# Token-major gates and merge, and transposes by 32x32 blocks and DMA over DRAM, in a hybrid encoder block

## The chip, the cores and the metric

The kernel runs on one core of a Trainium2 chip. The metric is the device time of one execution in microseconds (us); lower is better. The median of the runs shown is 1886.4 us. Everything is computed in float32 precision; the large products are done as three products of split operands (see below).

## The reference

The block takes `x` (256 tokens, 2048 channels) and computes, with one weight matrix `w_in` for all first projections:

```python
proj = h @ w_in                      # q, k, v, r, af, ab, hy_u, gate_logits
y_gla = gated_linear_attention(q, k, v, r, af, ab)     # 4 heads, both directions
y_hy = hyena(hy_u)                   # short conv, then two long convolutions by FFT
g = sigmoid(gate_logits)             # two gates of 2048 channels
merged = g[0] * (y_gla @ w_gla_o) + g[1] * (y_hy @ w_hy_o)
h = layernorm(ALPHA * h + merged @ w_out)
ff = square(relu(h @ w_ff1)) @ w_ff2                   # 2048 -> 8192 -> 2048
out = layernorm(ALPHA * h + ff)
```

## The kernel before

**Products.** Each activation is kept as `act[128, kt, 2, 256]`: channels on partitions (16 tiles `kt` of 128 channels), a high and a low part, and 256 tokens. `split_hi_lo` (L107) makes the parts: a cast on ScalarE (L108) and a subtraction on VectorE (L109). Weights arrive in 305 blocks of 128 x 2048 numbers in the order of use (`wblk`, built by `_layout`), each as one DMA on SP's queue, and are split in two halves in the same way (`fetch`, L115). There is room for three raw blocks and three split halves. A product is high x high + high x low + low x high.

There are two forms of product:
- `channel_pair` (L175): the weights are the stationary operand and the activation moves. A block holds 128 output channels by all 2048 inputs. It takes 16 matmuls of 512 columns (high and low activations side by side) and 16 of 256. The result has channels on partitions; the two sides are added by `channel_sum` (L169): a copy on ScalarE (L172) and an addition on VectorE (L173).
- `token_group` (L202): the activation is stationary and the weights move. Four blocks hold 512 outputs, and each block takes 24 matmuls of 512 columns. The result has tokens on partitions, in two PSUM banks, ready to use.

**Stages, in order.** First gates and filters: ga, q, k (channel), r (token), with the filters of Hyena computed on the side. Then v (token) with the GLA heads on the side: `gla_gates`, `gla_scores`, `gla_out` (L587). Then g1, the first gate (channel), whose sigmoid is applied in place after the GLA pool is closed (L642). Then the Hyena stage: eight chunks of 256 channels, each with three channel pairs uv, ux, uz, and, spread by `go_after` (L754), the eight channel pairs go of `y_gla @ w_gla_o`. Then g2 (channel), ho (`y_hy @ w_hy_o`, channel, merged into `mT`), wo (token), layer norm, and the MLP: ff1 in quarters (channel, L969), ff2 in quarters (token, L996), in the order f0, f1, w0, f2, w1, f3, w2, w3.

**Side work.** `later(d, fn)` puts a function on a list; `pump()` is called once per weight block and runs what is due, so `d` counts blocks from the call. Within what is written, the order of each engine is set by a planner that works with its own costs for every instruction and DMA; on the chip each engine then takes its instructions in that order. TensorE, VectorE, ScalarE, and the DMA queues of SP, ScalarE and POOL are all such in-order queues.

**Transposes.** Four places turn a tile between channels and tokens on partitions, each with four or eight 128x128 TensorE transposes against an identity into a side PSUM bank: `yt` in `gla_out` (L608), `vt` and `x1t` in `to_tokens` (L660), `yT` at the end of `hy_inv` (L737). These are 32 transposes each.

**Hyena chunk.** `hy_v` splits the turned v; `hy_fwd` loads the filter `Tl` from DRAM on POOL's queue and makes the forward transform `Zp`; `hy_mul` (L698) is the product in the frequency domain on VectorE; `hy_inv` the inverse `yp`, multiplied with x1 (order 0) or x2 (order 1). The result `yo` goes to DRAM (`yd`, L741) and comes back before ho as `yr` (L782).

Of the kernel before, what the change touches and what calls it, by code (L numbers as in the profile page):

```python
# [10 lines left out]
F32 = mybir.dt.float32  # L11
F32R = mybir.dt.float32r
I32 = mybir.dt.int32
AF = mybir.ActivationFunctionType
# [45 lines left out]
def block_kernel(  # L60
# [151 lines left out]
    def rsqrt_eps(dst, src, scale, pool, name, between=lambda: None):  # L212
# [4 lines left out]
        eng.scalar.activation(y, t, AF.Exp, scale=-0.5)  # L217
# [4 lines left out]
        eng.vector.tensor_tensor(dst, y, t, op=ALU.mult)  # L222

# [363 lines left out]
    def gla_out(h):  # L587
        def run():
            sth, stl = hst.pop(("st", h))
            vh, vl = v_sb.pop(h)  # L590
            y = gp.tile([P, NT, 512], F32, tag="y", name=f"y{h}")
            for ib in range(NT):
                po = psum_side(f"o{h}{ib}")
                for jb in range(NT):
                    cs = slice(ib * P, (ib + 1) * P)
                    mm3(po, sth[:, jb, cs], stl[:, jb, cs], vh[:, jb], vl[:, jb], jb == 0, jb == 1)
                ss = gp.tile([P, 1], F32, tag="ss", bufs=2, name=f"ss{h}{ib}")
                rs = gp.tile([P, 1], F32, tag="rsd", bufs=2, name=f"rs{h}{ib}")
                nc.scalar.activation(y[:, ib, :], po, AF.Square, accum_out=ss)
                rsqrt_eps(rs, ss, 1.0 / 512.0, gp, f"rq{h}{ib}")  # L600
                nc.vector.scalar_tensor_tensor(
                    y[:, ib, :], po, rs, g_sb[:, ib, h * 512:(h + 1) * 512], op0=ALU.mult, op1=ALU.mult)
            for k2 in range(2):
                pt = psum_side(f"yt{h}{k2}")
                for kk in range(2):
                    for ib in range(NT):
                        kt = 2 * k2 + kk
                        nc.tensor.transpose(  # L608
                            pt[:, kk * L + ib * P:kk * L + (ib + 1) * P],
                            y[:, ib, kt * P:(kt + 1) * P], ident)  # L610
                s = slice(4 * h + 2 * k2, 4 * h + 2 * k2 + 2)
                split_hi_lo(yT[:, s, 0], yT[:, s, 1], pt.rearrange("p (a b) -> p a b", a=2))
        return run

    for h in range(HEADS):
# [9 lines left out]
        later(1, gla_out(h))  # L625
# [3 lines left out]
        qp.tile([P, 8, L], F32, tag="q", name="m0"),  # L629
        qp.tile([P, 8, L], F32, tag="k", name="m1"),  # L630
    ]

    def m_pair(c2):
        return m_sb[c2 // 4][:, 2 * (c2 % 4):2 * (c2 % 4) + 2, :]

    for c2 in range(8):
        channel_pair(xT, f"g1_{c2}", m_pair(c2))
    drain()
    gstk.close()
    for c2 in range(8):  # L640
        mp = m_pair(c2)
        nc.scalar.activation(mp, mp, AF.Sigmoid)  # L642
# [17 lines left out]
    def to_tokens(src, name):  # L660
        pt = psum_side(name)
        for c in range(2):
            for tb in range(NT):
                nc.tensor.transpose(pt[:, tb * CW + c * P:tb * CW + (c + 1) * P], src[:, c, tb * P:(tb + 1) * P], ident)
        return pt.rearrange("p (a b) -> p a b", a=2)
# [5 lines left out]
    def hy_v(c):  # L671
        def run():
            z = z_tiles(f"{c}0")
            split_hi_lo(z[0], z[1], to_tokens(cst.pop(("v", c)), f"vt{c}"))
            cst[("z", c, 0)] = z
        return run

    def hy_x1(c):
        def run():
            x1 = hp.tile([P, NT, CW], F32, tag="x1", name=f"x1_{c}")  # L680
            nc.scalar.copy(x1, to_tokens(cst.pop(("x1c", c)), f"x1t{c}"))
            cst[("x1", c)] = x1
        return run
# [34 lines left out]
    def hy_inv(c, o):  # L718
        def run():
# [5 lines left out]
            if o == 0:  # L725
                zf = hp.tile([P, NT, CW], F32, tag="zf", name=f"zf{c}")
                nc.vector.tensor_tensor(zf, py3, cst.pop(("x1", c)), op=ALU.mult)
# [3 lines left out]
            else:  # L731
                zf = hp.tile([P, NT, CW], F32, tag="zf", name=f"zg{c}")
                nc.scalar.copy(zf, py3)
                pt = psum_side(f"yT{c}")
                for cc in range(2):
                    for tb in range(NT):
                        nc.tensor.transpose(pt[:, cc * L + tb * P:cc * L + (tb + 1) * P], zf[:, tb, cc * P:(cc + 1) * P], ident)  # L737
                yo = hp.tile([P, 2, L], F32, tag="zf", name=f"yo{c}")
                nc.vector.tensor_tensor(yo, pt.rearrange("p (a b) -> p a b", a=2), cst.pop(("x2", c)), op=ALU.mult)
                yd = drp.tile([P, 2, L], F32, tag=f"yd{c}", name=f"yd{c}")  # L740
                nc.gpsimd.dma_start(yd, yo)  # L741
                yh_dram[c] = yd
# [4 lines left out]
    def gla_o_pair():  # L747
        c2 = go_done[0]
        go_done[0] += 1
        ps = channel_pair(yT, f"go{c2}")  # L750
        mp = m_pair(c2)
        nc.vector.tensor_tensor(mp, mp, ps, op=ALU.mult)

    go_after = [0, 0, 1, 1, 1, 1, 1, 3]  # L754
    for c in range(NCH):
# [14 lines left out]
        for _ in range(go_after[c]):  # L770
            gla_o_pair()
# [403 lines left out]
```

## Time and profile before

| | |
|---|---|
| median of three runs | 1886.4 us (1885.57 to 1888.03) |
| profiled execution, span from first to last instruction | 1881.2 us |
| TensorE busy | 1862.4 us (99%), 9852 matmuls |
| VectorE busy | 1313.7 us (70%) |
| ScalarE busy | 948.2 us (50%) |
| POOL | 30.8 us (2%), 61 instructions |
| DMA | 375 MB, mean 199 GB/s |

The page of the profile gives for the profiled execution its span alone; the median of the runs is 5.2 us above it. "Busy" is the time in which an engine executes something. A row of the windows gives, for a stretch of the span, the busy time and the instruction count of each engine in order PE (matmul), PEld (weight load), DVE (VectorE), ACT (ScalarE), POOL, then the granted TensorE clock as a share of full speed, the busy share of the DMA engines and GB/s. A row of the chain in order of time has start, duration and what ran. A row of a group has the line, the engine, the operation, output and input, shapes and count, then the busy time, the mean of one in ns, and the idle time of the engine in front of it with what ended it. A row of the timeline has start, duration, engine, line, operation, and in brackets the idle time in front and what ended it. A row of the waits has who waited for whom, the total, the times and the longest.

### The profile page before, as it was taken

What the parts mean: (1) busy time and instruction counts of PE and PEld (TensorE: products, weight loads), DVE (VectorE), ACT (ScalarE), POOL (GpSimd) and SP (SyncE); (2) the same over time, 40 slices, a digit from 0 to 9 for tenths busy, and PEclk for the clock granted to TensorE, in tenths of its full rate; (3) what the DMA queues carried; (4) which work ended last, traced back from release to release, by engine and by line L of the source; (5) the groups of instructions that cost most, each with busy time, mean ns of one, the idle gap of its engine ahead of it and who ended that gap; (6) DMA issues with size and microseconds to landing.
All of it is one profiled execution on the core that took longest, in us unless ns stands there. A gap on an engine that the chain in (4) does not pass through costs nothing.

```text
span 1881.2 us, 24912 instructions
## 1 busy us (share of the span) xinstructions
PE 1862.4 (99%) x9852; PEld 1594.2 (85%) x9852; DVE 1313.7 (70%) x1709; ACT 948.2 (50%) x1278; POOL 30.8 (2%) x61
## 2 busy tenths in 40 slices
PE   8999999989999999999999999999999999999998
PEld 7888888878888888888888888888888888888887
DVE  6888878865788899888646667666555654665556
ACT  5555557674555555555544444544434443443332
POOL 1000000000000000000000000000000000000000
PEclk9999999999999999999999999999999999999999
DMA  8667664425455555555545662645554545454553
GB/s 289 226 228 281 231 252 153 178 90 212 183 193 196 209 204 197 196 210 195 222 186 195 262 253 104 233 180 197 183 199 186 198 179 201 185 195 182 198 190 124
DMA packets 60549, 375.05 MB, mean 199 GB/s; under 512 B 6832, under 2 KB 9552, under 8 KB 21008
## 3 DMA queue, kind: packets, MB, share of 16 engines
q1 hardware_dynamic: 47376, 324.03, 46.5%
q0 software_dynamic: 6288, 30.16, 4.5%
q10 hardware_dynamic: 6768, 19.27, 2.8%
q8 instruction: 77, 1.26, 0.3%
q14 instruction: 40, 0.33, 0.0%
HBM read 356.66 MB, written 16.78 MB: 199 GB/s over the span
## 4 chain that ended last, share of the span: by engine, by line
PE 95%; DVE 2%; ACT 1%; DMA 1%; issue 0%; SPq 0%; DVEq 0%; ACTq 0%
PE f L93 19%; PE w L93 19%; PE g L93 9%; PE uv L93 5%; PE go L93 5%; PE ho L93 5%; PE uz L93 5%; PE ux L93 5%; PE r L93 5%; PE v L93 4%; PE wo L93 4%; PE k L93 2%; PE q L93 2%; PE Zp L93 1%; PE yp L93 1%; PE s L93 1%
## 5 line engine op out<-in xcount | busy, mean ns | idle before, releaser
L109 DVE TENSOR_TENSOR wlo<-raw,whi 128x1024 fp32r<-128x1024 f32 (+2 forms) x603 | 729.1, 1211 | 467.3 <-ACT whi L108 451.0
L108 ACT CAST whi<-raw 128x1024 fp32r<-128x1024 f32 (+2 forms) x603 | 627.3, 1041 | 765.2 <-PE w L93 188.5
L93 PE MATMUL w<-whi,f 128*128 128x512 f32 x960 | 296.2, 389 | 0.0
L93 PE MATMUL f<-hT,whi 128*128 128x512 f32 x1000 | 250.7, 392 | 0.0
L93 PEld LDWEIGHTS w<-whi,f 128*128 128x128 f32 x960 | 180.2, 188 | 37.4
L93 PEld LDWEIGHTS f<-hT,whi 128*128 128x128 f32 x1000 | 179.8, 189 | 32.3 <-ACT whi L108 0.2
L93 PE MATMUL w<-wlo,f 128*128 128x512 f32 x480 | 186.8, 389 | 0.0
L93 PEld LDWEIGHTS f<-hT,wlo 128*128 128x128 f32 x1000 | 136.3, 190 | 9.7
L93 PE MATMUL f<-hT,wlo 128*128 128x256 f32 x1000 | 139.5, 282 | 0.0
L93 PE MATMUL g<-xT,whi 128*128 128x512 f32 x512 | 130.0, 395 | 3.7 <-DVE vl L109 3.7
L93 PEld LDWEIGHTS g<-xT,whi 128*128 128x128 f32 x512 | 92.6, 190 | 20.6 <-DVE vl L109 4.1
L93 PEld LDWEIGHTS w<-wlo,f 128*128 128x128 f32 x480 | 90.1, 188 | 18.6
L93 PE MATMUL r<-whi,xT 128*128 128x512 f32 x256 | 82.3, 391 | 0.0
L93 PE MATMUL v<-whi,xT 128*128 128x512 f32 x256 | 79.7, 390 | 0.0
L93 PEld LDWEIGHTS g<-xT,wlo 128*128 128x128 f32 x512 | 70.8, 192 | 5.1
L93 PE MATMUL g<-xT,wlo 128*128 128x256 f32 x512 | 72.6, 284 | 0.0
L93 PE MATMUL ux<-xT,whi 128*128 128x512 f32 x256 | 65.7, 394 | 0.0
L93 PE MATMUL uz<-xT,whi 128*128 128x512 f32 x256 | 65.6, 394 | 0.0
L93 PE MATMUL uv<-xT,whi 128*128 128x512 f32 x256 | 65.3, 394 | 0.0
L93 PE MATMUL go<-yg,whi 128*128 128x512 f32 x256 | 64.9, 393 | 0.0
L93 PE MATMUL wo<-whi,mT 128*128 128x512 f32 x208 | 64.2, 389 | 0.0
L93 PE MATMUL ho<-yh,whi 128*128 128x512 f32 x256 | 64.1, 392 | 0.0
(336 smaller groups left out, 2709.0 us busy)
## 6 DMA issues: line engine op xcount, KB each, us to landing
raw<-wblk SPq DMA_DIRECT2D x302, 1024.0 KB, 4.8
Td<-T POOLq DMA_DIRECT2D x16, 768.0 KB, 4.4
Tl<-Td POOLq DMA_DIRECT2D x16, 768.0 KB, 4.5
w<-w4s ACTq DMA_DIRECT2D x16, 512.0 KB, 5.1
zr<-ln_rows ACTq DMA_DIRECT2D x4, 1024.0 KB, 10.9
raw<-wblk SPq DMA_DIRECT2D x11, 256.0 KB, 7.0
dec<-decay_in ACTq DMA_DIRECT2D x8, 256.0 KB, 2.8
yd<-yo POOLq DMA_DIRECT2D x8, 256.0 KB, 4.5
```

Of the source, the lines that this page charges most:

```text
L93: return eng.tensor.matmul(*args, **kw)
L108: nc.scalar.copy(hi, src)
L109: nc.vector.tensor_tensor(lo, src, hi.bitcast(F32), op=ALU.subtract)
```

## The change

Five products change from the channel form to the token form: g1, go, g2, ho, and ff1 but for the first four blocks of its first quarter. `_layout` lays their weights out accordingly. The gates and the merge (`m_sb`, `g2_sb`) then have tokens on partitions, and the sigmoid of g1 is taken straight from PSUM, ordered behind the last GLA norm so that ScalarE changes its table once.

What is computed with tokens on partitions and needed with channels (the merged `mT`, the MLP's `f`), and the four places of TensorE transposes, are turned in another way: VectorE transposes a 128x512 tile in 32x32 blocks (`turn_blocks`), one DMA writes it to DRAM (`bounce_out`), and four DMAs, one for each 32 partitions, read it back with the blocks rearranged (`bounce_in`), in runs of 512 bytes. All of these DMAs are issued on POOL's queue. The splits of the returned tile are put off by `later`.

In the Hyena stage v, x1 and the final y are bounced in each chunk; due times move from 1, 3, 5, 6, 8 to 3, 4, 5, 6, 7 and 9 blocks, and `hy_x1` is gone, since x1 is used as it comes back. `go_after` counts groups of four blocks now. `gla_out` is cut into its two halves of 128 tokens, due one and two blocks after v.

```diff
+    def turn_blocks(st, src):
+        nc.vector.transpose(st, src.rearrange("p k (b i) -> p b k i", b=4))
+
+    def bounce_out(name, st, n):
+        td = drp.tile([n, P, 512], F32, tag=f"tr_{name}", name=f"tr_{name}")
+        nc.gpsimd.dma_start(td.rearrange("t p x -> p t x"), st)
+        return td
+
+    def bounce_in(sg, td):
+        src = td.rearrange("t (a i) (b x) -> b i (t a) x", a=4, b=4)
+        for b in range(4):
+            nc.gpsimd.dma_start(sg[32 * b:32 * b + 32], src[b])
...
+            yt = gp.tile([P, 4, 4, 32], F32, tag="yt", name=f"yt{h}{ib}")
+            turn_blocks(yt, y.rearrange("p (k x) -> p k x", k=4))
+            y_dram[h, ib] = bounce_out(f"y{h}{ib}", yt.rearrange("p b k j -> p (b k j)")[:, None, :], 1)
...
-        later(1, gla_out(h))
+        for ib in range(NT):
+            later(1 + ib, gla_out(h, ib))
...
-    for c2 in range(8):
-        channel_pair(xT, f"g1_{c2}", m_pair(c2))
+    for g in range(4):
+        pss = token_group(xT, f"g1_{g}")
+        for tb in range(NT):
+            sig = nc.scalar.activation(m_part(g, tb), pss[tb], AF.Sigmoid)
+            dep = mybir.DependencyInfo(mybir.DependencyClass.NoSync, mybir.DependencyReason.DATA)
+            tc.add_manual_dep(sig.ins, last_norm[0].ins.name, dep, reason="one table change")
+        for h, ib in ((g, 0), (g, 1)):
+            later(3 + ib, gla_back(h, ib))
...
+    def turned(src, name, tag):
+        st = hp.tile([P, 4, 4, 32], F32, tag="st", name=f"st{name}")
+        turn_blocks(st, src)
+        td = bounce_out(name, st.rearrange("p b k j -> p (b k j)")[:, None, :], 1)
+        sg = hp.tile([P, 4, P], F32, tag=tag, name=f"sg{name}")
+        bounce_in(sg, td)
+        return sg.rearrange("p a (k j) -> p k a j", k=4)
...
-    go_after = [0, 0, 1, 1, 1, 1, 1, 3]
+    go_after = [0, 0, 1, 0, 1, 0, 1, 1]
     for c in range(NCH):
         ps = channel_pair(xT, f"uv{c}")
-        cst[("v", c)] = short_conv(ps, 2 * c, f"cv{c}", "cv", 2)
-        later(1, hy_v(c))
-        later(3, hy_fwd(c, 0))
-        later(3, hy_mul(c, 0))
+        cst[("v", c)] = turned(quarters(short_conv(ps, 2 * c, f"cv{c}", "cv", 2)), f"v{c}", "sg")
+        later(3, hy_v(c))
+        later(4, hy_fwd(c, 0))
+        later(4, hy_mul(c, 0))
         ps = channel_pair(xT, f"ux{c}")
-        cst[("x1c", c)] = short_conv(ps, 16 + 2 * c, f"cx{c}", "cx", 1)
-        later(1, hy_x1(c))
+        cst[("x1", c)] = turned(quarters(short_conv(ps, 16 + 2 * c, f"cx{c}", "cv", 2)), f"x{c}", "x1")
...
-        later(8, hy_inv(c, 1))
+        later(7, hy_inv(c, 1))
+        later(9, hy_out(c))
...
+    for g in range(4):
+        pss = token_group(yhT, f"ho{g}")
+        st = hp.tile([P, NT, 512], F32, tag=("Z", "pa")[g % 2], name=f"mt{g}")
+        for tb in range(NT):
+            gp2 = g2_sb[:, tb, g * 512:(g + 1) * 512]
+            mp = m_part(g, tb)
+            nc.vector.tensor_tensor(gp2, gp2, pss[tb], op=ALU.mult)
+            nc.vector.tensor_tensor(mp, mp, gp2, op=ALU.add)
+            turn_blocks(st[:, tb].rearrange("p (b k j) -> p b k j", b=4, k=4), mp.rearrange("p (k x) -> p k x", k=4))
+        sg = hp.tile([P, 8, P], F32, tag=("Tl", "pb")[g % 2], name=f"mg{g}")
+        bounce_in(sg, bounce_out(f"m{g}", st, NT))
+        later(2, lambda g=g, sg=sg: back_split(mT[:, 4 * g:4 * g + 4], sg))
+    drain()
...
+        for g in range(1 if qi == 0 else 0, 4):
+            pss = token_group(hT, f"f{qi}{g}")
+            for tb in range(NT):
+                r, st = work[:, tb], work[:, 2 + tb]
+                nc.scalar.activation(r, pss[tb], AF.Relu)
+                nc.vector.tensor_tensor(r, r, r, op=ALU.mult)
+                turn_blocks(st.rearrange("p (b k j) -> p b k j", b=4, k=4), r.rearrange("p (k x) -> p k x", k=4))
+            sg = back[:, turns[0] % 2]
+            turns[0] += 1
+            bounce_in(sg, bounce_out(f"f{qi}{g}", work[:, 2:4], NT))
+            later(2, lambda g=g, sg=sg, f=f: back_split(f[:, 4 * g:4 * g + 4], sg))
```

More of the change, by code (lines that the diff above doesn't have):

```diff
@@ L585, in gla_scores, with gla_out @@
         return run
-    def gla_out(h):
+    y_dram = {}
+    last_norm = [None]
+    def gla_out(h, ib):
         def run():
[L589 to L612, printed above, removed]
@@ L672, in run @@
         def run():
[L673 to L682, printed above, removed]
+            zh, zl = z_tiles(f"{c}0")
+            sg = cst.pop(("v", c))
+            for tb in range(NT):
+                hi, lo = (t[:, tb].rearrange("p (c a j) -> p c a j", c=2, a=4) for t in (zh, zl))
+                split_hi_lo(hi, lo, sg[:, tb::2])
+            cst[("z", c, 0)] = (zh, zl)
         return run
```

147 lines of the change are left out of this document (86 added, 61 removed).

## The prediction

> **What bounds the kernel now.** I read the page first: the shares of the engines, then the chain of waits.
>
> ```profile
> span 1881.2 us, 24912 instructions
> PE 1862.4 (99%) x9852; PEld 1594.2 (85%) x9852; DVE 1313.7 (70%) x1709; ACT 948.2 (50%) x1278; POOL 30.8 (2%) x61
> PE 95%; DVE 2%; ACT 1%; DMA 1%; issue 0%; SPq 0%; DVEq 0%; ACTq 0%
> ```
>
> TensorE is busy for all but 18.8 us, and 95% of the chain runs through it. So the time is the sum of what TensorE executes, as long as the others keep its weights coming. What they must hold out is read by stage, from the windows (columns: busy time and count of PE, PEld, DVE, ACT, POOL, then granted clock, DMA share, GB/s). The five rows are the r stage, two of the Hyena stage, ff2(0) and ff1(2).
>
> ```profile
> 127.00:253.50 126.50, 126.50 (x573) 104.12 (x572) 104.56 (x151) 69.43 (x90) 5.31 (x10) 1.00 0.69 252
> 474.00:587.00 113.00, 113.00 (x643) 98.80 (x642) 91.94 (x117) 64.13 (x92) 2.14 (x4) 1.00 0.52 196
> 587.00:884.00 297.00, 297.00 (x1684) 259.31 (x1683) 264.94 (x316) 162.54 (x229) 10.72 (x20) 1.00 0.54 200
> 1342.40:1429.50 87.10, 87.10 (x386) 72.11 (x385) 44.79 (x42) 33.68 (x34) 0.00 (x0) 1.00 0.52 193
> 1429.50:1518.80 89.30, 89.30 (x514) 78.60 (x513) 54.14 (x63) 42.53 (x55) 0.00 (x0) 1.00 0.51 190
> ```
>
> TensorE never idles there and its granted clock is full. VectorE has 40% to spare in the MLP, but only 53 of 410 us (410.0 - 91.94 - 264.94) in the Hyena stage. That is the stage in which a load moved to VectorE can be felt.
>
> **1. Matmuls: -17.7 us.** The chain in order of time gives whole stages in both forms:
>
> ```profile
> 975.48 89.39 PE ho L93 x512
> 1342.44 87.07 PE w L93 x384
> 1429.51 89.36 PE f L93 x512
> ```
>
> Each is 16 weight blocks. A channel block is 16 matmuls of 512 columns and 16 of 256; a token block is 24 of 512. The columns are the same, 12288, so the gain is a quarter fewer instructions: (89.36 - 87.07) / 16 = 0.143 us a block. Turned are 16 blocks each of g1, go, g2, ho and 60 of 64 of ff1: 124 x 0.143 = 17.7 us. The three stages agree within 0.03 us, so I take it whole.
>
> The Trainium skill, "TensorE: Matmul & The Clock Gate", section "Wait — 56ns, not 53.3ns?", gives a start-to-start time of N / 2.4 GHz plus about 2.5 ns, 215.7 ns at 512. This trace has 87.07 / 384 = 226.7 ns, so it does not agree. By the page's figures a turned block would save an estimated 0.02 us and all of them 2.6 us; the sum would be 15 us worse. That result is the fourth rival below.
>
> **2. Transposes off TensorE: -14.1 us, and -1.2 us of wait.**
>
> ```profile
> 502.27 1.39 PE Zp L93 x6
> 503.66 0.22 PE x1t L664 x2
> PE yt L608 <- DVE y L601: 1.2, 1, 1.2
> PE g L93 <- DVE vl L109: 3.7, 1, 3.7
> ```
>
> Two transposes take 0.22 us of the chain, 0.11 each. Gone are 32 each of yt, vt, x1t and yT: 128 x 0.11 = 14.1 us, 96 of them (10.6 us) in the Hyena stage. The wait of yt for VectorE goes with them. The 3.7 us wait lies in the burst of GLA work at 380 us, which the change cuts into halves with a pump between; I leave it, and take its removal as the bound on the good side.
>
> The Trainium skill, "VectorE: DVE Perf Modes", section "Rules for kernel authors", would leave a 128x128 transpose on TensorE where PSUM will do as destination, and so speaks against this part. By that rule the sum would lack these 14.1 us and all that stands in 3 to 5 for the 32 transposed GLA and Hyena tiles.
>
> **3. VectorE's new load: nothing outside Hyena.** VectorE's transpose does not occur in this trace. The nearest rows:
>
> ```profile
> L250 DVE MEMSET wu<- 128x512 f32 x1 | 0.5, 485 | 0.1
> L752 DVE TENSOR_TENSOR m<-m,go_s 128x512 f32<-128x512 f32 x8 | 5.5, 687 | 0.0
> L109 DVE TENSOR_TENSOR wlo<-raw,whi 128x1024 fp32r<-128x1024 f32 x590 | 721.0, 1224 | 461.3 <-ACT whi L108 445.1 <-PE go L93 4.5 <-PE ux L93 3.3
> L173 DVE SCALAR_TENSOR_TENSOR go_s<-go,go_l 128x256 f32<-128x256 f32 x16 | 6.7, 419 | 0.0
> ```
>
> 512 elements cost 0.485 us (only written) to 1.22 (if each went through twice); I take 0.69, the pass that reads and writes 512. There are 70 of them: 8 in GLA, 24 in Hyena, 8 in ho, 30 in ff1. Against them go 124 channel sums at 0.419 us, since a token group is read straight out of PSUM. In ff1 a group loses four sums, two squares and two subtractions and gets two squares, two transposes and one subtraction of 1024: about -4.4 and +4.0 us, so the 35 us of spare VectorE in the ff1 row hide it. In g1 and ho it is as even.
>
> In Hyena VectorE gets 24 x 0.69 = 16.6 us, plus 24 x (2 x 0.42 - 0.69) = 3.6 for operations that are now done in halves (v's subtraction, zf, yo), less 16 x 0.419 = 6.7 for go: 356.9 + 13.5 = 370.4 us. TensorE needs 410 - 10.6 - 2.3 = 397.1. Spare VectorE falls from 53 to 26.7 us, still positive. At 1.22 us a transpose it would be 14.
>
> **4. The way over DRAM: +4.5 us in ff1, +5 us in Hyena.** A bounce is one DMA out and four in, all on POOL's queue: 51 bounces, 255 issues. The trace has one such round trip, yd out, yr in, and the cast of yr on ScalarE:
>
> ```profile
> 909.80 0.54 POOL L741 DMA_DIRECT2D yd<-yo  x1 [4.43 <-DVE yo L739]
> 913.33 0.54 POOL L782 DMA_DIRECT2D yr<-yd  x1 [2.99 <-DMA yd<-yo]
> 918.35 0.62 ACT L108 CAST yh<-yr 128x512 fp32r<-128x512 f32 x1 [3.85 <-DMA yr<-yd]
> 141.75 1.06 ACT L108 CAST whi<-raw 128x1024 fp32r<-128x1024 f32 x1
> 147.08 0.62 ACT L372 CAST wa<-w 128x512 fp32r<-128x512 f32 x1 [4.27 <-DMA w<-w4s]
> 148.23 1.04 ACT L108 CAST whi<-raw 128x1024 fp32r<-128x1024 f32 x1
> ```
>
> It takes 8.55 us. Four loads 0.54 apart add 1.6, so a bounce takes about 10.2. ScalarE was put at that cast 3.85 us too early: the planner expects a DMA sooner than it lands. What such a hold stops are the weight casts behind it on ScalarE, and VectorE's low parts behind those. The last three rows show what TensorE bears: two weight casts 6.48 us apart in the r stage, where it is busy for 126.50 of 126.50 us. In ff1 there lies the hold, a copy of 1024 (1.05) and the cast (1.05) between two casts, so about 4.4 us of hold are free. The work is due two blocks (10.9 us) after its group; relu, two squares and two transposes take 3.4 us, so the tile lands at 13.6: 2.7 us of hold if taken when due, 3.85 + 1.6 = 5.5 at the most. I take 4.7, nearer the yd row, so 0.3 us of stall: 15 x 0.3 = 4.5 us, bounds 0 and 16.
>
> In Hyena, v lands about 14 us after its block (2.4 us of convolution and the rest as above) and is due after three blocks, 16.8; y lands after 10.9 and is due after 11.2. So no hold if taken when due, 3.85 if taken as early as yr was. VectorE's spare 26.7 us over 16 holds (v and y; x1 has five blocks) bear 1.67 each. I take 2.0: 32 - 26.7 = 5 us, bounds 0 and 35. On POOL the T load of the next transform queues behind each load that waits for its store; it may, for those loads are issued about every 24 us.
>
> ```profile
> 787.55 0.53 POOL L688 DMA_DIRECT2D Tl<-Td  x1 [24.34 <-DVE pb L707]
> 805.39 0.53 POOL L688 DMA_DIRECT2D Tl<-Td  x1 [17.31 <-DVE pb L707]
> q0 software_dynamic: 6288, 30.16, 4.5%
> raw<-wblk SPq DMA_DIRECT2D x302, 1024.0 KB, 4.8
> ```
>
> The bounces move 70 x 256 KB twice, 36 MB, on queues half idle. At q0's bytes per share that is 5% of the span; at q0's time per packet (4.5% of 16 x 1881 us / 6288 = 0.215 us) with 512-byte packets it is 26%. Either fits beside a share of 0.5 to 0.7, and a weight block has 10.9 us for its 4.8; so nothing is charged.
>
> **5. From ho to wo: +2 us.** The last ho group now needs 4.1 us (two times multiply, add, transpose), 10.2 of bounce and 2.3 of split: 16.6 us. wo0 needs those rows of mT at its fourth block, after 3 x 5.44 = 16.3 us. That hides it but for 0.3; ScalarE, held meanwhile in front of wo's casts, may add up to 5.5. I take 2, bounds 0 and 6. Elsewhere (f0 to f3, yg) a stage of 16 blocks or more lies between. The sigmoids of g1, now straight from PSUM and behind the last GLA norm, cost ScalarE less than the low copies that go (it is at 50%).
>
> **Sum.** -17.7 - 14.1 - 1.2 + 4.5 + 5 + 2 = -21.5. The profiled execution's span of 1881.2 becomes 1859.7; the median of the runs shown, 1886.4, lies 5.2 us above that span, and what lies around it does not change: **1865 us**. Without any stall it is 1853, with the middle of the upper bounds 1878.
>
> **Rivals.**
> - **VectorE becomes the bound in Hyena (slower).** One mechanism: VectorE stands at v's and y's returned tiles. From 1.67 us a hold it prices TensorE; from (26.7 + 5 + 21.5) / 16 = 3.3 us the gain is gone. At the 3.85 us of the yr row: 61.6 - 26.7 = 35 us, 30 more than I took: 1895 us. For it: that row, and VectorE at 89% in the 587 to 884 window. Against it: the due times are later than the landings.
> - **ScalarE's holds in ff1 and ho eat the gain (no change).** At 5.5 us each, 19 x 1.1 = 21 us instead of 6.5, and a little more in Hyena: 1865 + 14.5 + 5 = 1885. For it: due 10.9, landing 13.6. Against it: TensorE bore 6.48 us between casts.
> - **All is hidden and the GLA burst goes too (better).** 1853 less the 3.7 us: 1849.
> - **A token block is not cheaper here.** If the 0.143 us belonged to the stage and not to the form, 15 us of part 1 would be missing: 1880 us. Against it: ho and f, different stages, have the same 89.4.
>
> **How the numbers follow.** Forecast 0.58, VectorE bound 0.15, no change 0.10, better 0.10, token block not cheaper 0.07. A measurement of this kernel tells about 0.2%, 3.8 us, from no change. Faster: 0.55 of the forecast, 0.10 better, 0.07 of the last: 0.72. Same: 0.03 of the forecast and 0.08 of no change: 0.11. Slower: 0.15 and 0.02: 0.17. The range reaches from the better case to just under the VectorE case: 1848 to 1893; the forecast's own is 1853 to 1878.
>
> **What would show it.** ff1(2) should take 87.1 us in the windows and ho 87.1. The Hyena stage should shrink from 410 to about 402 us with VectorE above 90%; the longest waits of VectorE and ScalarE for a DMA should name sg and back, below 5 us each. A VectorE transpose of 128x512 near 0.69 us. The forecast is wrong if TensorE idles by more than 35 us in all, or if a token block takes 5.58 us.

## The result, and the profile after

The changed kernel takes **1856.1 us** (median of four runs, 1853.6 to 1859.1) against 1886.1 us for the kernel before on the same chip: a ratio of 0.984, 95% interval 0.983 to 0.986. The forecast was 1865 us, in a range of 1848 to 1893. The page of the profile after:

```profile
span 1855.3 us, 22858 instructions
PE 1834.9 (99%) x8732; PEld 1531.8 (83%) x8732; DVE 1311.4 (71%) x1660; ACT 913.8 (49%) x1152; POOL 177.7 (10%) x316
q0 software_dynamic: 19328, 66.88, 11.8%
```

TensorE lost 27.5 us of work (1862.4 to 1834.9) and its idle time grew from 18.8 to 20.4 us. The last row is the queue of POOL's DMAs: 66.88 MB instead of 30.16, for 11.8% of the DMA engines' time instead of 4.5%. The windows of the kernel before, for the three stretches that the prediction did not quote (from the end of v to the end of g1; Hyena with g2; from the end of ho to the layer norm):

```profile
359.90:473.70 113.80, 107.61 (x644) 94.03 (x644) 73.25 (x130) 68.86 (x113) 0.53 (x1) 0.99 0.44 156
473.70:975.48 501.78, 501.78 (x2851) 438.91 (x2850) 412.45 (x496) 275.06 (x385) 16.62 (x31) 1.00 0.54 200
1064.87:1176.38 111.51, 109.00 (x536) 91.74 (x535) 74.00 (x106) 50.39 (x64) 0.00 (x0) 0.98 0.57 215
1176.63:1870.06 693.43, 693.43 (x3562) 594.15 (x3561) 402.97 (x446) 298.48 (x348) 0.00 (x0) 1.00 0.51 190
```

The last row is the MLP (f0 to w3, from where its matmuls run without a gap). The same four stretches of the changed kernel, then its Hyena stage without g2 and its f2:

```profile
360.50:461.30 100.80, 100.79 (x492) 83.75 (x491) 71.65 (x116) 59.53 (x96) 21.34 (x39) 1.00 0.64 219
461.30:947.99 486.69, 486.24 (x2498) 416.16 (x2497) 415.43 (x511) 256.43 (x345) 83.47 (x151) 1.00 0.67 232
1035.50:1159.00 123.50, 114.08 (x535) 93.65 (x534) 79.78 (x112) 54.17 (x65) 3.05 (x5) 0.96 0.56 204
1159.47:1844.11 684.64, 684.64 (x3082) 569.46 (x3081) 399.20 (x401) 296.52 (x303) 45.79 (x75) 1.00 0.62 215
461.30:854.20 392.90, 392.45 (x2084) 338.49 (x2083) 345.04 (x441) 209.41 (x291) 69.13 (x125) 1.00 0.67 230
1408.24:1495.28 87.04, 87.04 (x385) 72.07 (x385) 50.80 (x50) 40.38 (x42) 9.17 (x15) 1.00 0.67 230
```

Between these marks every microsecond can be placed. "Predicted" is the sum of the prediction's own terms for that stretch.

| stretch | before | after | change | predicted |
|---|---|---|---|---|
| start to the end of v | 359.9 | 360.5 | +0.6 | 0 |
| end of v to the end of g1 | 113.8 | 100.8 | -13.0 | -7.0 (16 blocks, 32 transposes, yt's wait) |
| Hyena and g2 | 501.8 | 486.7 | -15.1 | -10.2 (-15.2, and 5 of stall) |
| ho | 89.4 | 87.5 | -1.9 | -2.3 |
| end of ho to the MLP | 111.8 | 124.0 | **+12.2** | +2 |
| MLP | 693.4 | 684.6 | -8.8 | -4.1 (-8.6, and 4.5 of stall) |
| rest | 11.1 | 11.2 | 0 | 0 |
| span | 1881.2 | 1855.3 | -25.9 | -21.5 |

So the sum came out 4.4 us off, but as a difference of larger misses: one step cost 10.2 us more than forecast, three brought 15.6 us more (6.0, 4.9 and 4.7), and the rest adds up to 1.0.

The VectorE transposes by form, then, from the view of the waits, the longest holds at returned tiles and what TensorE waited for in wo:

```profile
L203 DVE STREAM_TRANSPOSE work<-work 128x512 f32<-128x512 f32 x30 | 21.3, 711 | 1.0
L203 DVE STREAM_TRANSPOSE sty<-yp 128x512 f32<-128x512 f32 x8 | 5.7, 707 | 0.0
```

```profile
ACT f L108 <- DMA back<-tr_f: 17.3, 13, 3.0
ACT mT L108 <- DMA mg<-tr_m: 15.5, 4, 6.5
ACT zh L108 <- DMA sgv<-tr_v: 6.7, 4, 2.9
DVE yo L768 <- DMA sgy<-tr_y: 6.1, 5, 2.5
PE wo L93 <- ACT whi L108: 3.7, 3, 1.5
```

A row of the waits reads: total, number of times, longest; a "hold" is the time for which an engine stands at a tile that has not come back. In ff1 and Hyena the holds exist but are short (1.3 us each at back), and TensorE works for 684.64 of 684.64 us in the MLP and for 486.24 of 486.69 in Hyena and g2: they cost nothing there. Between ho and wo they do cost. The chain of waits there, and ScalarE's and VectorE's timeline at its start:

```profile
1044.71 9.81 DMA tr_m<-mt
1056.79 6.46 DMA mg<-tr_m
1064.45 53.06 PE wo L93 x226
```

```profile
1035.09 1.04 ACT L108 CAST mT<-mg 128x1024 fp32r<-128x1024 f32 x1 [6.49 <-DMA mg<-tr_m]
1036.17 1.22 DVE L109 TENSOR_TENSOR mT<-mg,mT 128x1024 fp32r<-128x1024 f32 x1 [6.31 <-ACT mT L108]
1037.31 2.35 DVE L109 TENSOR_TENSOR wlo<-raw,whi 128x1024 fp32r<-128x1024 f32 x2
1039.58 1.28 DVE L828 TENSOR_TENSOR g_sb<-g_sb,ho 128x512 f32<-128x512 f32 x2
1063.36 1.04 ACT L108 CAST mT<-mg 128x1024 fp32r<-128x1024 f32 x1 [0.96 <-DMA mg<-tr_m]
```

ho's matmuls end at 1035.50. ScalarE has just stood 6.49 us for the tile of the third group; VectorE's subtraction for it and two low parts are ahead of the last merge, which starts at 1039.58. Its store leaves at 1044.71, and ScalarE starts on the returned tile at 1063.36: 27.9 us after ho's end, where the prediction had 14.3 (4.1 and 10.2; its 16.6 takes in the split that follows).

### The profile page after: what moved, and what is told of

Same layout as the page of the kernel before. It is cut to its first block, busy times and chain, and to the rows that moved or that the text cites. A ratio compares the mean times of both kernels' runs of the same rounds, so it can differ in the third digit from the quotient of the medians.

```text
span 1855.3 us, 22858 instructions
## 1 busy us (share of the span) xinstructions
PE 1834.9 (99%) x8732; PEld 1531.8 (83%) x8732; DVE 1311.4 (71%) x1660; ACT 913.8 (49%) x1152; POOL 177.7 (10%) x316
## 3 DMA queue, kind: packets, MB, share of 16 engines
q0 software_dynamic: 19328, 66.88, 11.8%
## 4 chain that ended last, share of the span: by engine, by line
PE 59%; issue 4%; DMA 3%; DVE 2%; POOL 1%; ACT 0%; DVEq 0%; ACTq 0%; POOLq 0%
PE w L93 19%; PE f L93 18%; PE g L93 5%; PE go L93 4%; PE wo L93 3%; PE ux L93 2%; PE uz L93 2%; PE uv L93 2%; DMA tr_m<-mt 1%; PE ho L93 1%; PE Zp L93 1%; PE yp L93 1%; DMA mg<-tr_m 1%; PE wo L49 0%; PE f L49 0%
## 5 line engine op out<-in xcount | busy, mean ns | idle before, releaser
L93 PE MATMUL f<-whi,hT 128*128 128x512 f32 x960 | 296.1, 389 | 0.0
L93 PEld LDWEIGHTS f<-whi,hT 128*128 128x128 f32 x960 | 180.2, 188 | 37.4
L93 PE MATMUL f<-wlo,hT 128*128 128x512 f32 x480 | 186.7, 389 | 0.0
L93 PE MATMUL g<-whi,xT 128*128 128x512 f32 x512 | 158.3, 389 | 0.0
L93 PEld LDWEIGHTS g<-whi,xT 128*128 128x128 f32 x512 | 96.1, 188 | 20.0
L93 PEld LDWEIGHTS w<-wlo,f 128*128 128x128 f32 x480 | 90.1, 188 | 18.7
L93 PEld LDWEIGHTS f<-wlo,hT 128*128 128x128 f32 x480 | 90.1, 188 | 18.6
L93 PE MATMUL g<-wlo,xT 128*128 128x512 f32 x256 | 99.9, 390 | 0.0
L93 PE MATMUL go<-whi,yg 128*128 128x512 f32 x256 | 79.8, 389 | 0.0
L93 PE MATMUL ho<-whi,yh 128*128 128x512 f32 x256 | 79.0, 389 | 0.0
L207 POOL DMA_DIRECT2D tr_f<-work x15 | 10.9, 725 | 523.2 <-DVE work L203 523.2
```

The lines of the kernel that those rows point to most:

```text
L93: return eng.tensor.matmul(*args, **kw)
L207: nc.gpsimd.dma_start(td.rearrange("t p x -> p t x"), st)
```

## The experiments

The first theory was: the parts that remove work (matmuls, transposes) are worth what was summed; what is lost lies between ho and wo, where late returns hold ScalarE. Its rivals were that the bounces disturb the weight supply everywhere (then each stage loses a little), and that VectorE's new load is felt in Hyena. All runs stand against the kernel before, measured on the same chip; "ho to MLP" goes from ho's first matmul to where the MLP runs closed, "MLP" from there to w3's end, both in the profiled execution.

| kernel | median (us) | ratio, 95% interval | ho to MLP | MLP |
|---|---|---|---|---|
| before | 1883 to 1886 | 1 | 201.2 | 693.4 |
| changed | 1856.1 | 0.983 to 0.986 | 211.5 | 684.6 |
| loads_behind | 1853.5 | 0.983 to 0.986 | 209.0 | 685.2 |
| merge_first | 1860.0 | 0.986 to 0.990 | 209.9 | 690.8 |
| gla_whole | 1861.4 | 0.986 to 0.989 | 213.5 | 689.5 |
| hyena_dve_24 | 1865.6 | 0.988 to 0.993 | 212.0 | 690.5 |
| hyena_on_pe | 1881.6 | 0.996 to 1.000 | 211.0 | 698.3 |
| casts_late | 1859.9 | 0.986 to 0.989 | 203.5 | 698.2 |
| hyena_on_pe_casts_late | 1885.8 | 0.997 to 1.003 | 217.2 | 705.4 |
| ho_late | 1856.0 | 0.982 to 0.987 | 204.3 | 695.0 |
| ff1_channel | 1866.8 | 0.989 to 0.992 | 210.3 | 693.4 |
| ho_late_f_halves | 1849.9 | 0.981 to 0.984 | 211.5 | 684.6 |
| all_halves | 1850.6 | 0.982 to 0.985 | 204.6 | 684.6 |
| halves_only | 1906.9 | 1.011 to 1.014 | | |

**hyena_on_pe: Hyena's transposes back on TensorE.** v, x1 and y as before, with the due times of before; all else as changed.

```diff
-        cst[("v", c)] = turned(quarters(short_conv(ps, 2 * c, f"cv{c}", "cv", 2)), f"v{c}", "sg")
-        later(3, hy_v(c))
+        cst[("v", c)] = short_conv(ps, 2 * c, f"cv{c}", "cv", 2)
+        later(1, hy_v(c))
...
-                cst[("y", c)] = turned(py.rearrange("p (k x) -> p k x", k=4), f"y{c}", "sg")
+                        nc.tensor.transpose(pt[:, cc * L + tb * P:cc * L + (tb + 1) * P], zf[:, tb, cc * P:(cc + 1) * P], ident)
```

> The changed kernel with the Hyena stage's transposes put back on TensorE with their due times of before (v, x1 and the last y; 96 transposes), so 24 bounces fewer; go, g1, g2, ho and ff1 stay in the token form. Theory: the transposes cost TensorE 0.11 us each and VectorE had room for its share, so the Hyena stage and g2 grow by 10.6 us: 1866.5 us (1864 to 1869), without new idle time of TensorE. Rival, that VectorE's load or the holds at returned tiles cost the changed kernel something in this stage: the difference is smaller, 0 to 7 us: 1856 to 1863.

Its Hyena stage and g2:

```profile
462.30:960.35 498.05, 497.47 (x2594) 425.57 (x2593) 403.77 (x464) 265.68 (x353) 16.72 (x31) 1.00 0.57 201
```

They take 498.1 us instead of 486.7: 11.4 us for 96 transposes, where the sum had 10.6. But the whole kernel is some 25 us slower than the changed one, which neither theory nor rival allowed for, and 13.6 of that lies in the MLP, whose code was not touched. That was the surprise which the later runs follow.

**halves_only: the kernel before with only `gla_out` cut in halves**, due at 1 and 2, its transposes on TensorE.

```diff
-        later(1, gla_out(h))
+        for ib in range(NT):
+            later(1 + ib, gla_out(h, ib))
```

> The kernel before with one thing of the change: gla_out cut into its two halves of 128 tokens, due one and two blocks after v, its transposes still on TensorE. In the changed kernel the stretch from the end of v to the end of g1 is 13 us shorter (113.8 to 100.8), of which 7.0 are matmuls, transposes and the wait for yt; 6 are left over, and TensorE's idle time there went from 6.2 us to nothing. Theory: the cut spreads the burst, so 4 to 6 us of it come with the cut alone: 1881 us (1879.5 to 1882.5). Rival: what frees ScalarE and VectorE there is the token form of g1 (no low copies, no channel sums), and the cut alone gives nothing: 1885 to 1887.

It is 23 us slower than before, where both theory and rival had 1887 at most. The waits say where; the prediction shows what stood in these two places before, 1.2 us at yt and 3.7 in front of g (there for vl):

```profile
PE yt L604 <- DVE y L600: 10.4, 2, 5.8
PE g L93 <- DVE m L173: 8.1, 1, 8.1
```

Cutting the burst does not relieve it as long as TensorE itself makes the transposes and so stands for a half's y.

**gla_whole: the changed kernel with both halves due together.**

```diff
-            later(1 + ib, gla_out(h, ib))
+            later(1, gla_out(h, ib))
```

> The changed kernel with both halves of gla_out due one block after v again. The cut alone, on the kernel before, cost 22 us, since TensorE stood before the transposes of each half (10.4 us at yt and 8.1 at the next g). Theory: what took TensorE's idle time out of the GLA stage in the changed kernel is that nothing on TensorE follows the norms any more, with g1 in the token form; the cut matters little there: 1854 to 1858. Rival: the cut spreads the burst and is worth the 6 us: 1859 to 1863.

The stretch from v to g1 takes 100.9 us, as in the changed kernel. With halves_only this says that the spreading bought nothing there. What is left as the cause of the gain is that TensorE no longer stands behind y, and that g1 needs no channel sums on VectorE; the two were not separated. As a time the kernel fell among the rival's 1859 to 1863, but the 5 us that it is slower lie again in the MLP (689.5 us for 684.6), which this edit does not touch.

**hyena_dve_24: every Hyena transpose done twice on VectorE**, 24 more at 0.71 us, 17 us.

```diff
-        turn_blocks(st, src)
+        for _ in range(2):
+            turn_blocks(st, src)
```

> The changed kernel with every Hyena transpose on VectorE done twice into the same tile: 24 more of 0.706 us, 17 us more VectorE work in the stage. The trace of the changed kernel shows VectorE at 345.0 of 392.9 us there, 48 us spare. Theory (VectorE is not the bound, the weak rival of the prediction stays false): 0 to 2 us more, 1854 to 1858. Rival, that VectorE is the bound at returned tiles: 8 to 17 us more, 1863 to 1873.

Its windows and the one wait that is new there:

```profile
460.60:952.70 492.10, 488.66 (x2497) 418.05 (x2496) 429.38 (x533) 256.30 (x344) 82.15 (x149) 0.99 0.66 228
```

```profile
PE uv L93 <- DVE m L783: 3.4, 1, 3.4
```

Of 17 us more work on VectorE, Hyena and g2 lose 5.4 (492.1 for 486.7), where 0 to 2 were expected; 3.4 of them are one stand behind the go merge. The time of the whole, 1865.6, fell among the rival's 1863 to 1873, but 5.9 us of it lie in the MLP. So the changed kernel is not bound by VectorE in Hyena, but its margin is smaller than 17 us.

**loads_behind and merge_first: two ways at the gap before wo.** The first puts the loads of x and of the layer-norm rows, which start at 1035.7 on ScalarE's queue, behind the last return on POOL's. The second gives the merges and stores of ho priority over the weight work.

```diff
-    nc.scalar.dma_start(z1, x.rearrange("(a p) d -> p a d", p=P))
+    load_behind(z1, x.rearrange("(a p) d -> p a d", p=P))   # on POOL's queue, behind the last bounce_in
```

> The changed kernel with one thing moved: the loads of x and of the first two layer-norm rows (4 MB as they land) go from ScalarE's queue, where they start as ho ends, to POOL's queue behind the last bounce. In the changed kernel the time from the end of ho to the last of the layer-norm matmuls of f is 123.5 us, against 111.5 before, and the last store tr_m takes 9.8 us to land against 3.8 for the others. Theory: those loads crowd the last bounce; then the last tr_m lands in about 4 us, wo waits 6 us less and runs less at the low clock, and the time is 1849 us (1846 to 1852). Rival: the wait comes from VectorE, which takes the last merge 4 us late, and from ScalarE standing at the tile before; then tr_m still lands late or the stall stays, and the time is 1854 to 1858. It may also lose: if x comes too late for the first sum of wo, 1858 or more.

```diff
+            with tc.high_priority():
                 nc.vector.tensor_tensor(gp2, gp2, pss[tb], op=ALU.mult)
...
+        with tc.high_priority():
+            bounce_in(sg, bounce_out(f"m{g}", st, NT))
```

> The changed kernel with the merges of ho (multiply, add, transpose) and their bounces at high priority in the planner; nothing else. Theory of VectorE's lateness: the last merge starts within 1 us of the end of ho instead of 3.9 us after it, the last bounce is out about 4 us sooner, and of the 12 us lost between ho and the layer norm about 5 go: 1851 us (1848 to 1853). Rival, that the crowded store sets the end: the store starts sooner but lands in about 10 us still, and the time falls by at most 2: 1854 to 1857.

With the loads behind, the last store lands in 3.8 us instead of 9.8, but its four returns take 8.1 us at the median (6.7 in the changed kernel) and TensorE waits 5.6 us for mT: most of the delay only moved, and the time did not change. With priority the last merge starts 3.8 us after ho's last matmul, 4.1 in the changed kernel: what stands in front of it, the subtraction for the held tile, is released no earlier. The kernel is slower, and the loss lies in the MLP (6.2 us).

**casts_late: take the returned tiles later, in ho and in ff1.** They are cast one block later and behind the weight cast issued last, and x is loaded behind the last of them.

```diff
-        later(2, lambda g=g, sg=sg: back_split(mT[:, 4 * g:4 * g + 4], sg))
+        later(3, lambda g=g, sg=sg: back_split(mT[:, 4 * g:4 * g + 4], sg, True))
+    wo0 = token_group(mT, "wo0")
...
-    nc.scalar.dma_start(z1, x.rearrange("(a p) d -> p a d", p=P))
+    queue_behind(nc.scalar.dma_start(z1, x.rearrange("(a p) d -> p a d", p=P)), back_cast[0])
...
-            later(2, lambda g=g, sg=sg, f=f: back_split(f[:, 4 * g:4 * g + 4], sg))
+            later(3, lambda g=g, sg=sg, f=f: back_split(f[:, 4 * g:4 * g + 4], sg, True))
```

> The changed kernel with the casts of the returned tiles of ho and ff1 put later in ScalarE's order: due three blocks after the group instead of two and queued behind the last weight cast fetched by then, so that seven weight casts instead of five stand between the second relu (or the merge) and the cast. The last merge's cast comes inside the first group of wo, and the loads of x and of the first layer-norm rows stand behind it on ScalarE. Theory: a hold of ScalarE at a returned tile is what loses time, in ff1 once it passes about 4 us and at ho to wo, where the loads of x only choose which of the two last DMAs is late. Without holds the waits of ScalarE for back and mg vanish, wo starts without a gap, the 12 us lost between ho and the layer norm shrink to 3 or less: 1846 us (1843 to 1850), all runs within 3 us. Rival: the last merge's round trip itself is longer than three blocks of wo: then TensorE waits at the fourth block whatever ScalarE does, and it is 1851 to 1855.

Half of it held: ho to MLP falls to 203.5 us. The MLP went against the theory: it is 13.6 us longer, and ScalarE stands at back for 31.1 us in all, 17.3 in the changed kernel. The stores of ff1 also land later, 6.1 us at the median where the changed kernel has 3.7 (both rows for 1160 to 1680 us, casts_late first):

```profile
tr_f<-work POOLq DMA_DIRECT2D x15, 512.0 KB, 6.1
tr_f<-work POOLq DMA_DIRECT2D x15, 512.0 KB, 3.7
```

**hyena_on_pe_casts_late**, hyena_on_pe with the late casts in ff1 alone, was to take the 13.6 us away:

> The kernel with the Hyena transposes on TensorE, with nothing else but the late casts in ff1 (as in casts_late, ff1 only). That kernel took 1881.6 us with runs from 1870 to 1886, though its ff1 instructions stand in the same order on ScalarE as in the changed kernel; in its trace the holds at back come to 52.5 us against 16.4, and ff1 to ff2 take 13 us more. Theory: the holds in ff1 keep themselves up from group to group, and are the 13 us; with the casts late the time is 1867 us (1864 to 1870) with a spread below 4 us. Rival: the time was lost by the Hyena stage's transposes or by a clash of DMAs that does not depend on where the cast stands: 1876 to 1884.

It did not; the MLP grew to 705.4 us, and its stores landed in 6.0 us at the median. So taking the tile later was the wrong cure.

**ho_late: the late casts in ho alone**, with ff1 exactly as changed.

```diff
-        later(2, lambda g=g, sg=sg: back_split(mT[:, 4 * g:4 * g + 4], sg))
+        later(3, lambda g=g, sg=sg: back_split(mT[:, 4 * g:4 * g + 4], sg, True))
+    wo0 = token_group(mT, "wo0")
...
+    queue_behind(nc.scalar.dma_start(z1, x.rearrange("(a p) d -> p a d", p=P)), back_cast[0])
```

> The changed kernel, with three things done otherwise between ho and wo and nothing done otherwise in the MLP: ho's returned tiles are cast one block later and behind a weight cast, the last merge's return is no longer forced in front of wo0, and x and the first layer-norm rows are loaded behind the last returned tile. If the 12 us by which the stretch from ho's end to the end of the layer norm's matmuls grew (111.5 to 123.5) belong to ScalarE standing in front of wo's casts, that stretch takes 116 to 117 us, as in the run with late casts in both places, and with the MLP left alone the kernel takes 7 us less than the changed one: ratio about 0.981 to before. If the MLP falls into late casts whatever is done in front of it, f0 to w3 take 8 to 13 us more than the changed kernel's 685 us, and the ratio is 0.985 to 0.988.

The gap closes again (204.3), but not the 7 us follow: the profiled execution gives 10.4 back in an untouched ff1 (695.0). Here the chain of waits shows what happens in ff1, one round of four that look alike; then rows of the timeline (ScalarE, POOL) for the same round, and the wait in all:

```profile
1272.40 8.03 PE f L93 x34
1281.90 1.33 POOL back L220 x3
1283.63 9.54 DMA back<-tr_f
1293.27 1.06 ACT f L110
1295.50 1.23 DVE wlo L111
1296.77 8.03 PE f L93 x34
```

```profile
1268.90 1.05 ACT L110 CAST f<-back 128x1024 fp32r<-128x1024 f32 x1 [5.30 <-DMA back<-tr_f]
1271.75 0.59 ACT L1048 ACTIVATE work<-f 128x512 f32<-128x512 f32 x1
1277.58 0.72 POOL L214 DMA_DIRECT2D tr_f<-work  x1 [16.73 <-DVE work L210]
```

```profile
ACT f L110 <- DMA back<-tr_f: 42.8, 12, 6.3
```

It is a closed ring. ScalarE stands 5.3 us for a returned tile (the "fetch" below is its four loads, from the first one's issue to the cast). Behind that cast, in order, are two weight casts, for which TensorE then waits, and the relu of the next group. So the relu is late (2.85 us after the cast), its tile leaves late (5.8 us on), is fetched late (4.3 us on), lands 11.4 us after that, and holds ScalarE again. A round takes (1320.36 - 1249.03) / 3 = 23.8 us over the three from this chain; a group's own work is 87.04 / 4 = 21.8. Each round loses 2 us, until a quarter of ff2, which returns no tiles, lets ScalarE get ahead. The same steps in the changed kernel, from its timeline (ScalarE, then POOL):

```profile
1255.28 0.60 ACT L1033 ACTIVATE work<-f 128x512 f32<-128x512 f32 x1 [0.98 <-PE f L93]
1270.51 1.05 ACT L108 CAST f<-back 128x1024 fp32r<-128x1024 f32 x1
```

```profile
1260.09 0.72 POOL L207 DMA_DIRECT2D tr_f<-work  x1 [15.13 <-DVE work L203]
1264.16 2.33 POOL L213 DMA_DIRECT2D back<-tr_f  x4 [3.34 <-issue]
```

```profile
1249.89 1.05 ACT L108 CAST f<-back 128x1024 fp32r<-128x1024 f32 x1 [1.04 <-DMA back<-tr_f]
1293.02 1.05 ACT L108 CAST f<-back 128x1024 fp32r<-128x1024 f32 x1 [0.64 <-DMA back<-tr_f]
```

From relu to store 4.8 us, to the fetch 4.1, to the cast at most 6.35, and nothing waits. The last two rows are the casts of the groups before and behind: there the fetch took 7.3 us (from 1242.63) and 6.9 (from 1286.08), ScalarE stood for 1.0 and 0.6 us, and TensorE for nothing. So the same instructions run in two ways, in the ring and out of it. The largest difference is the fetch, 11.4 us against about 7; with that one step short, the ring would close in less than 21.8 us and dissolve. What decides which way an execution goes was not isolated. merge_first, gla_whole, hyena_dve_24 and hyena_on_pe, with holds of 32 to 53 us at back in all, and the two kernels with late casts in ff1 run part of ff1 in the ring too: in the chain of waits over the MLP of each of these six the fetch of a returned tile stands 3 to 10 times, mostly one group after the other and 21 to 25 us apart.

**ff1_channel: the change without its ff1**, which is in channel form as before, with no bounces.

```diff
-            pss = token_group(hT, f"f{qi}{g}")
...
-            bounce_in(sg, bounce_out(f"f{qi}{g}", work[:, 2:4], NT))
+                r = channel_pair(hT, f"f{qi}_{c2}")
```

> The changed kernel with ff1 wholly in the channel form of before: no token blocks and no bounces in ff1. By the prediction's term the 60 blocks cost 0.143 us more each, 8.6 us; if the bounces of ff1 cost nothing in the changed kernel, this is 8.6 us slower than it: ratio about 0.989. If holds at the returned tiles ate half of that, as part 4 of the prediction had it (4.5 us), it is 4 us slower: 0.9865. If they cost more than the token form gains, this is the faster: below 0.984. f2 and f3 should take 89.4 us each.

Its f2 takes what it took before:

```profile
1409.66 89.36 PE f L93 x512
```

The MLP takes 693.43 us, to the last digit the time of before, and 8.8 more than the changed kernel. Out of the ring the bounces of ff1 cost nothing, and the term for the matmuls is whole. The ratio is 0.9907; the 0.989 that was expected lies at the edge of its interval.

**ho_late_f_halves and all_halves: make the return earlier instead of its use later.** The tile of ff1 goes out in two stores of 256 KB, each as soon as its 128 tokens are turned; in all_halves ho's as well. Both keep the late casts of ho.

```diff
+            td = drp.tile([NT, P, 512], F32, tag=f"tr_f{qi}{g}", name=f"tr_f{qi}{g}")
             for tb in range(NT):
...
+                nc.gpsimd.dma_start(td[tb], st)
-            bounce_in(sg, bounce_out(f"f{qi}{g}", work[:, 2:4], NT))
+            bounce_in(sg, td)
```

> As the kernel with the late casts between ho and wo, and in ff1 each half of 128 tokens goes to DRAM by a DMA of its own as soon as it is transposed, so that the first 256 KB start some 2 us earlier. If the returned tiles of ff1 are late because the store of 512 KB starts late and takes 4 to 6 us, they land 1 to 2 us earlier, ScalarE's holds at back fall below 10 us over all, and the MLP takes the changed kernel's 685 us or a little less: ratio 0.980 to 0.981. If the lateness is contention with the weight loads, which more DMAs do not lessen, the holds stay at 16 to 40 us and the MLP takes up to 13 us more.

> As the kernel with the late casts between ho and wo and the halved stores of ff1, and the merged tiles of ho also go to DRAM in two stores of 256 KB, each as soon as its half is transposed. If the returns of ho are late because the store of 512 KB starts late, they are waited for less: ScalarE stands for mg under 5 us in all (9.3 before), TensorE waits under 3 us for mT, the stretch from ho's end to the end of the layer norm's matmuls takes 114 to 118 us, f0 and f1 keep their 162 us, and the ratio is 0.979 to 0.981. If it is contention with the weight loads and with x, nothing changes: 0.982.

The MLP is back at 684.63 us in both, without a gap; ScalarE stands 3.6 and 4.2 us at back over all. ho_late_f_halves is ho_late but for that store: 3.6 us of hold against 42.8, in one profiled execution of each. From relu to fetch it needs 7.7 us (1253.49 to 1261.19), the changed kernel 8.9, the ring 10.2. In the first the gap before wo was open again in the profiled execution (211.5 us, a return of mg took 9.0), and the ratio was 0.9822 where 0.980 to 0.981 was expected; in the second, halved there too, it is 204.6. The rows of all_halves:

```profile
ACT f L110 <- DMA back<-tr_f: 4.2, 2, 2.2
ACT mT L110 <- DMA mg<-tr_m: 1.4, 1, 1.4
```

```profile
1151.85 161.73 PE f L93 x728
1313.58 87.04 PE w L93 x384
```

Its profiled span is 1847.7 us, 7.6 below the changed kernel's. Every stretch came out as expected, but not the ratio: 0.9833 where 0.979 to 0.981 was said. As a time it is not told apart from the changed kernel, 0.982 to 0.985 against 0.983 to 0.986; ho_late_f_halves, at 0.981 to 0.984, neither. Both beat the kernel before; that they beat the changed one is not shown. Nor is it shown that halved stores always keep the kernel out of the ring: seven of the nine profiled kernels that bounce ff1 in whole stores lose 4.8 to 20.8 us in the MLP and neither of the two with halves does, but the changed kernel and loads_behind keep out of it with whole stores too, and ho_late's own executions range from 1849.0 to 1858.4 us.

## Why the prediction was right, and where it was not

**Matmuls: right.** f2 takes 87.04 us where 87.1 was said, and the MLP's 8.8 us for 60 blocks are 0.147 each for the 0.143 taken. The rival "a token block is not cheaper" is out: ff1_channel gives the time back. The Trainium skill's 215.7 ns for such a matmul ("TensorE: Matmul & The Clock Gate", section "Wait — 56ns, not 53.3ns?") is still not met; 87.04 / 384 = 226.7 ns in the new stages too. (124 times the estimate of 0.02 us that the prediction worked out from it is 2.5 us, not 2.6.)

**Transposes: right.** 15.2 us were summed for Hyena and g2 with their blocks, 15.1 were gained, and undoing Hyena's part cost that stage 11.4 for 10.6. The Hyena stage alone was to shrink to 402 us and shrank to 392.9; 5 of these 9 us are the stall that did not come, and most of the rest is work of the last chunk that now runs beside g2 (g2 was to fall from 91.5 to 89.2 us and takes 93.8).

The Trainium skill's rule to leave such transposes on TensorE ("VectorE: DVE Perf Modes", section "Rules for kernel authors") was the slower choice here, by 11.4 us in that stage, with TensorE 99% busy and VectorE at 70%.

**VectorE: right in kind.** 0.69 to 0.71 us a transpose for 0.69. Over Hyena and g2 VectorE gained 3.0 us (412.45 to 415.43); the 13.5 of the prediction leave out the 16 channel sums that g2 loses (6.7 us), and were 4 too many beside. The "above 90%" did not come: 345.04 of 392.90 is 88%. The rival that VectorE's holds bind Hyena (1895 us) is out: holds at sgv and sgy are 12.8 us in all, 2.9 at the longest, and TensorE idles for 0.45. The longest hold of all is not at one of the tiles that the prediction named but at mg, 6.5 us.

**The way over DRAM: the mechanism right, its price by luck.** The prediction took 4.5 us in ff1 and 5 in Hyena, and the changed kernel shows 0 in both. For ff1 the step that failed is the hold of 4.7 us, taken between "2.7 us of hold if taken when due, 5.5 at the most", with each hold priced by itself: the changed kernel's are 1.3 us on the mean and 3.0 at the most, and holds are not independent. Out of the ring they cost nothing; in it each passes to the next group, and the kernels with this ff1 pay 4.8 to 13.6 us, inside the bounds of 0 and 16. With the late casts in ff1 as well it is up to 20.8.

**From ho to wo: the term that was mis-sized.** It said 2 us with bounds 0 and 6; it was 12.2; in the windows 6.9 of it are more idling and 5.1 longer matmuls, for which the prediction had no term (TensorE's granted clock is 0.79 in the second row below). Two of its numbers failed. The merge was to take 4.1 us from ho's end and starts only after that, behind the subtraction of a held tile and two low parts (store at 9.2 us after ho's end). And the bounce was to take 10.2 us, from a round trip in a stage whose DMA engines were 54% busy at 200 GB/s; here it took 18.7 (1044.71 to 1063.36). The window 1035.5 to 1055 shows why that is plausible, with x and the rows loaded beside weights (94% busy at 379 GB/s); in all_halves, which delays these loads, the same window is less full (its row stands last):

```profile
1035.50:1055.00 19.50, 17.08 (x73) 13.36 (x72) 14.17 (x15) 10.24 (x11) 0.72 (x1) 1.00 0.94 379
1055.00:1065.00 10.00, 6.17 (x15) 4.04 (x16) 3.02 (x3) 2.94 (x3) 2.33 (x4) 0.79 0.70 218
```

```profile
1035.50:1055.00 19.50, 17.84 (x78) 14.15 (x77) 12.10 (x13) 6.82 (x7) 3.47 (x6) 1.00 0.79 261
```

Moving the loads alone, to POOL's queue, did not help. The edit of ho_late (the later slot on ScalarE, wo's first group ahead of the last cast, and the loads behind it) took about 7 us off in three of its four profiled kernels (203.5, 204.3 and 204.6 us from ho to MLP) and nothing in the fourth (211.5); the six with ho as changed have 210.3 to 217.2. Which part of that edit carries it was not tried apart.

**GLA: better than said, by 6 us.** The 3.7 us wait that was left in, as the bound on the good side, is gone, and with it all 6.2 us that TensorE idled between v and the end of g1. Of the 6 us beyond the forecast 5.0 are this idling, less the 1.2 at yt that the sum had, and 1.0 is time in which TensorE worked. The cut into halves, which the prediction named beside it, is not the cause.

**The total: in part by luck.** In the span the forecast came within 4.4 us because overpriced holds (9.5 us) and an underpriced GLA gain (6.0) stood against an underpriced gap (10.2). The time itself missed by 8.9 us, and the other 4.5 are no part of the sum. The prediction carried over the 5.2 us by which the median before lay above the profiled span, as if they were something around the span; after, the median lies 0.8 us above it. In every execution with both on record the time is 1.7 to 1.9 us above its own span (1857.15 and 1855.3 us for the profiled one), so the larger part of the 5.2 was the distance between one execution and the median. The upper end of the forecast's own range, 1878, does not follow either: half of its upper bounds of 16, 35 and 6 us on 1853 is 1882.

What stays open is why the fetch takes long in the ring (its four loads landed in 6.5 us at the median between 1250 and 1275, 3.9 in the changed kernel), since the DMA engines' share over f0 and f1 is about the same (0.68 and 0.70). That it meets the weight loads at another moment is a guess that no run tested.

## What to carry to other kernels

Work taken off the bounding engine could be summed here from like stages, to 0.1 us in Hyena with g2 and to 0.2 in the MLP; a transfer's latency could not be taken from a place with half the traffic, and is to be measured where its neighbours load. Before a tile's return is put into an in-order queue that also carries the next group's weights and evictions, add the ring up: if the way from eviction to return and back to the next eviction can exceed one group's time, a lateness can be handed on from group to group. Then try to start the transfer earlier, in parts, before trying to use it later: here the first left no hold above 2.2 us at ff1's returned tiles in two profiled executions, and the second did not help.

## What was not expected of the hardware

- In the changed kernel a store of 512 KB landed in 3.5 to 4.1 us in ff1 and in 9.8 in the window where the DMA engines were 94% busy at 379 GB/s.
- In the 10 us in which TensorE stood for 3.8 its granted clock was 0.79, and in the 55 us behind it 0.98 (1.00 in the 19.5 us before): the stretch from ho to the MLP lost 5.1 us in longer matmuls (114.08 us busy against 109.00 for as many) and 6.9 in idling.
- One and the same program spread over 0.8% in ten executions (hyena_on_pe, 1869.9 to 1885.8 us) and over 1.0% (hyena_on_pe_casts_late, 1875.7 to 1895.0), where the kernel before, timed beside the first, stayed within 0.2%. The ring has the size for it, but which executions ran in it is known for the profiled ones alone.
